# Contrast adjustment in one pass over 48 images: equal 32 KB rows, six buffers, two hardware DMA queues, a sum shared by two engines and a clip in two chunks

## The chip, the cores and the metric

The kernel runs on one core of a Trainium2 chip; the other cores were not part of the program. The metric is the device time of one execution in microseconds (us), lower is better. A profiled execution gives a span, which is about 1.8 us shorter than the measured time (238.6 us against 240.4 us).

## The reference

```python
x: (16, 3, 512, 512) float32, uniform random in 0..1        # 48 images of 1 MB, 50.33 MB
mean = np.mean(x, axis=(2, 3), keepdims=True)
return np.clip(mean + factor * (x - mean), 0, 1).astype(np.float32)      # factor = 1.5
```

Every image has to be read whole before its first output can be computed. So 50.33 MB come in and 50.33 MB go out, and between load and store an image stays on chip.

## The kernel before

A tile holds four images: 128 partitions with 8192 float32 each, so that one row of the DMA is 32 KB. The last two tiles hold two images, with rows of 16 KB. VectorE sums each row, a small matmul with a block matrix adds the rows of one image and spreads `(1 - factor) * mean`, ScalarE forms `relu(factor * x + bias)`, VectorE takes the minimum with 1, and the tile is stored from where it lies. A framework orders the instructions and places the waits.

```python
TILE_IMGS = [4] * 11 + [2, 2]
X_BUFS = 5
...
    for i, N in enumerate(TILE_IMGS):
        ...
        nc.sync.dma_start(out=xt, in_=src)                       # load: SP's hardware queue
        nc.vector.tensor_reduce(out=rsum, in_=xt, axis=X, op=add)
        nc.tensor.matmul(pbias, blockw[N], rsum, start=True, stop=True)
        nc.scalar.copy(out=bias, in_=pbias)
        nc.scalar.activation(out=xt, in_=xt, func=Relu, bias=bias, scale=factor)
        nc.vector.tensor_scalar(out=xt, in0=xt, scalar1=1.0, scalar2=None, op0=min)
        nc.gpsimd.dma_start(out=dst, in_=xt)                     # store: Pool's software queue
```

## Time and profile before

| | before |
|---|---|
| time, median of the first 3 runs | 240.37 us (240.05 to 240.52) |
| span of the profiled execution | 238.6 us |
| VectorE busy, ScalarE busy | 156.5 us (66%), 89.1 us (37%) |
| bytes by DMA | 100.66 MB, 422 GB/s over the span |

The first view is the page of the kernel before. The span is cut into 40 equal slices; the digits are the busy share of a slice in tenths, and the last line gives GB/s by slice. Below come the two DMA queues (packets, MB, share of 16 engines' time) and the costliest instructions (count | busy us, mean ns | idle us before them, and what ended it).

```profile
DVE  0088999999599079459629909917945979742300
ACT  2002966472906601900920650470190095406000
DMA  7999999999999999999999999999999999999995
GB/s 269 434 439 439 439 439 352 439 434 439 439 439 439 439 434 434 423 428 412 423 439 439 434 439 439 439 439 439 434 428 426 426 404 428 431 434 439 428 434 214
...
q1 hardware_dynamic: 1872, 50.33, 49.4%
q0 software_dynamic: 1872, 50.33, 49.0%
...
L77 DVE TENSOR_REDUCE rsum<-xt 128x1 f32<-128x8192 f32 (+1 forms) x13 | 104.4, 8029 | 61.7 <-DMA xt<-in_x_dram 61.7
L90 ACT ACTIVATE xt<-xt,bias 128x8192 f32<-128x8192 f32 (+1 forms) x13 | 85.8, 6598 | 0.4
L97 DVE TENSOR_SCALAR xt<-xt 128x8192 f32<-128x8192 f32 (+1 forms) x13 | 53.2, 4091 | 5.0 <-ACT xt L90 5.0
```

The row to read is DMA: 9 in all but the first and the last slice. VectorE and ScalarE have gaps, and VectorE's are ended by loads. The waits of the DMA queue on SP say what the loads themselves wait for, namely stores, which free the buffers:

```profile
SPq L74 <- DMA out_dram<-xt: 186.4, 8, 58.2
```

The packet records of the trace sharpen this. A row of 32 KB is one packet there; its median duration is 1.213 us in both directions, which makes 16 x 32,768 B / 1.213 us = 432 GB/s. The first data packet starts at 1.75 us, the last ends at 236.81 us, and all packet durations together make 234.74 us per engine. So the DMA is full from end to end.

In the timeline of one tile in the steady state (start, duration, instruction), the order on VectorE is sum of tile t+1, then clip of tile t:

```profile
162.37 8.69 DVE L77 TENSOR_REDUCE rsum<-xt 128x1 f32<-128x8192 f32 x1 [6.34 <-DMA xt<-in_x_dram]
170.97 4.42 DVE L97 TENSOR_SCALAR xt<-xt 128x8192 f32<-128x8192 f32 x1
175.69 0.53 POOL L104 DMA_DIRECT2D out_dram<-xt  x1 [18.83 <-DVE xt L97]
```

The clip and store belong to the tile that landed one period (19.4 us) earlier: a tile is on chip for about 33 us between landing and store.

### The profile page before, as it was taken

Reading aid. Unit: us, or ns where it says so; the run is one execution under the profiler, and the core shown is the slowest. Engines: PE = TensorE matmul, PEld = TensorE weight load, DVE = VectorE, ACT = ScalarE, POOL = GpSimd, SP = SyncE. Lnnn points to the kernel's source line nnn. Section 1 sums busy time; section 2 is a strip of 40 time slices with the busy share of each in tenths; the row PEclk is TensorE's granted clock in tenths of the full one; section 3 lists DMA queues with packets and bytes.
Section 4 is the critical chain, followed back from the end, with each engine's and each line's share of the span. In section 5 each row is a group of like instructions: output and inputs, shape, how many; then the busy total and the mean of one; then the engine's idle time right before and its main releaser. Section 6 shows DMA issues by size and latency. Waiting matters only on the chain.

```text
span 238.6 us, 238 instructions
## 1 busy us (share of the span) xinstructions
PE 7.4 (3%) x26; PEld 6.5 (3%) x26; DVE 156.5 (66%) x26; ACT 89.1 (37%) x27; POOL 10.3 (4%) x25
## 2 busy tenths in 40 slices
PE   0000000000000000000000000000000000000000
PEld 0000000000000000000000000000000000000000
DVE  0088999999599079459629909917945979742300
ACT  2002966472906601900920650470190095406000
POOL 2000001000000000000000000000000000500000
DMA  7999999999999999999999999999999999999995
GB/s 269 434 439 439 439 439 352 439 434 439 439 439 439 439 434 434 423 428 412 423 439 439 434 439 439 439 439 439 434 428 426 426 404 428 431 434 439 428 434 214
DMA packets 3744, 100.66 MB, mean 422 GB/s; under 512 B 416, under 2 KB 416, under 8 KB 416
## 3 DMA queue, kind: packets, MB, share of 16 engines
q1 hardware_dynamic: 1872, 50.33, 49.4%
q0 software_dynamic: 1872, 50.33, 49.0%
HBM read 50.33 MB, written 50.33 MB: 422 GB/s over the span
## 4 chain that ended last, share of the span: by engine, by line
issue 38%; DMA 35%; DVE 18%; POOL 2%; POOLq 0%; SPq 0%
DMA xt<-in_x_dram 19%; DMA out_dram<-xt 16%; DVE rsum L77 11%; DVE xt L97 7%; POOL out_dram L104 2%; POOLq L137 0%; SPq L74 0%; POOLq L104 0%
## 5 line engine op out<-in xcount | busy, mean ns | idle before, releaser
L77 DVE TENSOR_REDUCE rsum<-xt 128x1 f32<-128x8192 f32 (+1 forms) x13 | 104.4, 8029 | 61.7 <-DMA xt<-in_x_dram 61.7
L90 ACT ACTIVATE xt<-xt,bias 128x8192 f32<-128x8192 f32 (+1 forms) x13 | 85.8, 6598 | 0.4
L97 DVE TENSOR_SCALAR xt<-xt 128x8192 f32<-128x8192 f32 (+1 forms) x13 | 53.2, 4091 | 5.0 <-ACT xt L90 5.0
L88 ACT COPY bias<-pbias 128x1 f32<-128x1 f32 x13 | 2.1, 160 | 130.6 <-PE pbias L85 130.6
L104 POOL DMA_DIRECT2D out_dram<-xt x13 | 9.0, 692 | 213.0 <-DVE xt L97 212.8
L85 PE MATMUL pbias<-rsum,blockw 128*128 128x1 f32 x26 | 7.4, 355 | 209.5 <-DVE rsum L77 209.5
L85 PEld LDWEIGHTS pbias<-rsum,blockw 128*128 128x128 f32 x26 | 6.5, 311 | 210.3 <-DVE rsum L77 107.1
L88 ACT ACT_TABLE_LOAD x1 | 1.3, 1283 | 0.8 <-PEq L123 0.8
L51 POOL MEMSET blockw<- 32x32 f32 (+1 forms) x6 | 0.8, 128 | 0.2
L49 POOL MEMSET blockw<- 128x128 f32 x2 | 0.3, 205 | 0.3 <-POOLq L123 0.3
L123 POOL MEMSET const-float32-0.0<- 128x1 f32 x1 | 0.1, 104 | 0.2 <-issue 0.2
L123 POOL MEMSET const-bfloat16-1.0<- 128x1 bf16 x1 | 0.1, 113 | 0.0
L123 POOL MEMSET const-uint8-127<- 128x1 uint8 x1 | 0.1, 113 | 0.0
L123 POOL MEMSET const-float32-1.0<- 128x1 f32 x1 | 0.1, 110 | 0.0
## 6 DMA issues: line engine op xcount, KB each, us to landing
xt<-in_x_dram SPq DMA_DIRECT2D x11, 4096.0 KB, 24.6
out_dram<-xt POOLq DMA_DIRECT2D x11, 4096.0 KB, 36.0
xt<-in_x_dram SPq DMA_DIRECT2D x2, 2048.0 KB, 19.5
out_dram<-xt POOLq DMA_DIRECT2D x2, 2048.0 KB, 19.1
```

The costliest lines, as they stand in the source:

```text
L49: nc.gpsimd.memset(wt, 0.0)
L51: nc.gpsimd.memset(wt[b * PPI : (b + 1) * PPI, b * PPI : (b + 1) * PPI], wconst)
L77: nc.vector.tensor_reduce(out=rsum, in_=xt, axis=mybir.AxisListType.X, op=mybir.AluOpType.add,)
L85: nc.tensor.matmul(pbias, blockw[N], rsum, start=True, stop=True)
L88: nc.scalar.copy(out=bias, in_=pbias)
L90: nc.scalar.activation(out=xt, in_=xt, func=mybir.ActivationFunctionType.Relu, bias=bias, scale=factor,)
L97: nc.vector.tensor_scalar(out=xt, in0=xt, scalar1=1.0, scalar2=None, op0=mybir.AluOpType.min,)
L104: store_eng.dma_start(out=dst, in_=xt)
L123: nc = _bacc.Bacc("TRN2", target_bir_lowering=False, num_devices=1)
```

## The change

The intent is to shorten each tile's stay on chip and to take Pool's software queue out of the path: the sum is shared (4352 columns on VectorE, 3840 on ScalarE at the same time), the scale and the clip overlap in two chunks, the stores go out by ScalarE's hardware queue, six buffers replace five, all tiles are equal, and the order of instructions is fixed by hand (`manual_schedule`). The diff, cut to its core:

```diff
-TILE_IMGS = [4] * 11 + [2, 2]
-X_BUFS = 5
+ROW = 8192
+BUFS = 6
+CHUNKS = (5120, 3072)
+SUM = 4352
...
-        nc.vector.tensor_reduce(out=rsum, in_=xt, axis=X, op=add)
-        nc.tensor.matmul(pbias, blockw[N], rsum, start=True, stop=True)
-        nc.scalar.copy(out=bias, in_=pbias)
-        nc.scalar.activation(out=xt, in_=xt, func=Relu, bias=bias, scale=factor)
-        nc.vector.tensor_scalar(out=xt, in0=xt, scalar1=1.0, scalar2=None, op0=min)
-        nc.gpsimd.dma_start(out=dst, in_=xt)
+        nc.vector.tensor_reduce(out=sums[:, 0:1], in_=xt[:, 0:SUM], axis=X, op=add)
+        nc.scalar.activation(out=junk, in_=xt[:, SUM:ROW], func=Copy, accum_out=sums[:, 1:2])
+        nc.tensor.matmul(pbias, blockw, sums[:, 1:2], start=True, stop=False)
+        nc.tensor.matmul(pbias, blockw, sums[:, 0:1], start=False, stop=True)
+        nc.vector.tensor_copy(out=bias, in_=pbias)
+        for n in CHUNKS:
+            part = xt[:, c : c + n]
+            nc.scalar.activation(out=part, in_=part, func=Relu, bias=bias, scale=factor)
+            nc.vector.tensor_scalar(out=part, in0=part, scalar1=1.0, scalar2=None, op0=min)
+            c += n
+        nc.scalar.dma_start(out=dram(out_f, t), in_=xt)
...
+    with tc.manual_schedule():
+        for t in range(min(BUFS, n_tiles)):
+            load(t)
+        for t in range(n_tiles):
+            compute(t)
+            store(t)
+            if t + BUFS < n_tiles:
+                load(t + BUFS)
```

More of the change, by code (lines that the diff above doesn't have):

```diff
@@ L5 @@
 import concourse.tile as tile
-from concourse import bass_utils, mybir
+from concourse import mybir
 from concourse._compat import with_exitstack
-TILE_IMGS = [4] * 11 + [2, 2]
-X_BUFS = 5
-STORE_ENGINE = "gpsimd"
+P = 128
+ROW = 8192
+BUFS = 6
+CHUNKS = (5120, 3072)
+SUM = 4352
 @with_exitstack
@@ L23 @@
     nc = tc.nc
-    P = 128
+    f32 = mybir.dt.float32
+    Alu = mybir.AluOpType
+    Act = mybir.ActivationFunctionType
     B, C, H, W = x.shape
-    n_img = B * C
-    n_pix = H * W
+    n_img, n_pix = B * C, H * W
+    ppi = n_pix // ROW
+    per_tile = P // ppi
+    n_tiles = n_img // per_tile
+    assert ppi * ROW == n_pix and per_tile * n_tiles == n_img
     factor = float(factor)
-    f32 = mybir.dt.float32
-    assert sum(TILE_IMGS) == n_img
-    NMAX = max(TILE_IMGS)
+    wconst = (1.0 - factor) / float(n_pix)
@@ L36, with dram @@
     x_f = x.rearrange("b c h w -> (b c h w)")
     out_f = out.rearrange("b c h w -> (b c h w)")
-    wconst = (1.0 - factor) / float(n_pix)
+    def dram(ap, t):
+        return bass.AP(tensor=ap.tensor, offset=t * P * ROW, ap=[[ROW, P], [1, ROW]])
     consts = ctx.enter_context(tc.tile_pool(name="consts", bufs=1))
-    blockw = {}
-    for N in sorted(set(TILE_IMGS)):
-        wt = consts.tile([P, P], f32, name=f"blockw{N}")
-        PPI = P // N
-        if N == 1:
-            nc.gpsimd.memset(wt, wconst)
-        else:
-            nc.gpsimd.memset(wt, 0.0)
-            for b in range(N):
-                nc.gpsimd.memset(wt[b * PPI : (b + 1) * PPI, b * PPI : (b + 1) * PPI], wconst)
-        blockw[N] = wt
@@ L54 @@
-    xpool = ctx.enter_context(tc.tile_pool(name="xpool", bufs=X_BUFS))
-    rpool = ctx.enter_context(tc.tile_pool(name="rpool", bufs=12))
-    bpool = ctx.enter_context(tc.tile_pool(name="bpool", bufs=12))
-    psum = ctx.enter_context(tc.tile_pool(name="psum", bufs=8, space=bass.MemoryType.PSUM))
-    if STORE_ENGINE == "sync":
-        store_eng = nc.sync
-    elif STORE_ENGINE == "act":
-        store_eng = nc.scalar
-    else:
-        store_eng = nc.gpsimd
-    pix_off = 0
-    for i, N in enumerate(TILE_IMGS):
-        FREE = n_pix * N // P
-        npix_tile = n_pix * N
-        xt = xpool.tile([P, NMAX * n_pix // P], f32, name="xt")[:, :FREE]
-        src = bass.AP(tensor=x_f.tensor, offset=pix_off, ap=[[FREE, P], [1, FREE]])
-        dst = bass.AP(tensor=out_f.tensor, offset=pix_off, ap=[[FREE, P], [1, FREE]])
-        nc.sync.dma_start(out=xt, in_=src)
-        rsum = rpool.tile([P, 1], f32)
+    xpool = ctx.enter_context(tc.tile_pool(name="xpool", bufs=BUFS))
@@ new lines, with load @@
+    jpool = ctx.enter_context(tc.tile_pool(name="jpool", bufs=1))
+    rpool = ctx.enter_context(tc.tile_pool(name="rpool", bufs=2))
+    bpool = ctx.enter_context(tc.tile_pool(name="bpool", bufs=2))
+    psum = ctx.enter_context(tc.tile_pool(name="psum", bufs=2, space=bass.MemoryType.PSUM))
+    blockw = consts.tile([P, P], f32, name="blockw")
+    nc.gpsimd.memset(blockw, 0.0)
+    for a in range(0, P, ppi):
+        nc.gpsimd.memset(blockw[a : a + ppi, a : a + ppi], wconst)
+    tiles = {}
+    def load(t):
+        xt = xpool.tile([P, ROW], f32, name="xt")
+        nc.sync.dma_start(out=xt, in_=dram(x_f, t))
+        tiles[t] = xt
@@ L77, with compute @@
+    def compute(t):
+        xt = tiles[t]
+        sums = rpool.tile([P, 2], f32, name="sums")
         nc.vector.tensor_reduce(
-            out=rsum,
-            in_=xt,
-            axis=mybir.AxisListType.X,
-            op=mybir.AluOpType.add,
-        )
-        pbias = psum.tile([P, 1], f32)
-        nc.tensor.matmul(pbias, blockw[N], rsum, start=True, stop=True)
-        bias = bpool.tile([P, 1], f32)
-        nc.scalar.copy(out=bias, in_=pbias)
+            out=sums[:, 0:1], in_=xt[:, 0:SUM], axis=mybir.AxisListType.X, op=Alu.add
+        )
+        junk = jpool.tile([P, ROW - SUM], f32, name="junk")
@@ L90 @@
         nc.scalar.activation(
-            out=xt,
-            in_=xt,
-            func=mybir.ActivationFunctionType.Relu,
-            bias=bias,
-            scale=factor,
-        )
-        nc.vector.tensor_scalar(
-            out=xt,
-            in0=xt,
-            scalar1=1.0,
-            scalar2=None,
-            op0=mybir.AluOpType.min,
-        )
-        store_eng.dma_start(out=dst, in_=xt)
-        pix_off += npix_tile
+            out=junk, in_=xt[:, SUM:ROW], func=Act.Copy, accum_out=sums[:, 1:2]
+        )
@@ new lines, in compute @@
+        pbias = psum.tile([P, 1], f32, name="pbias")
+        nc.tensor.matmul(pbias, blockw, sums[:, 1:2], start=True, stop=False)
+        nc.tensor.matmul(pbias, blockw, sums[:, 0:1], start=False, stop=True)
+        bias = bpool.tile([P, 1], f32, name="bias")
+        nc.vector.tensor_copy(out=bias, in_=pbias)
+        c = 0
+        for n in CHUNKS:
+            part = xt[:, c : c + n]
+            nc.scalar.activation(out=part, in_=part, func=Act.Relu, bias=bias, scale=factor)
+            nc.vector.tensor_scalar(out=part, in0=part, scalar1=1.0, scalar2=None, op0=Alu.min)
+            c += n
@@ L110, with store @@
+    def store(t):
+        nc.scalar.dma_start(out=dram(out_f, t), in_=tiles.pop(t))
+    with tc.manual_schedule():
[6 more added lines that the diff above has]
+                load(t + BUFS)
 _INS = ['x', 'factor']
```

## The prediction

> **What bounds the kernel now.** The DMA engines, nearly all of the time. The 40 slices show them 90% or more busy in 38 slices, at 404 to 439 GB/s in nearly all of them; the page's mean is 422 GB/s for 100.66 MB. In the trace's packet records the first data packet starts at 1.8 us of the 238.6 us span and the last ends at 236.8 us, and between 20 us and that end the 16 engines are 100% busy. The 32 KB packets take 1.213 us (median) in both directions: 16 x 32,768 B / 1.213 us is 432 GB/s. All packets together take 234.7 us per engine, so the DMA has no bubble to give back. VectorE is busy 156.5 us (66%), ScalarE 89.1 us (37%). In the waits, VectorE waits 61.7 us for loads, and the load queue 186.4 us for stores to free buffers.
>
> **What the change does.**
> - Sum: the VectorE reduce of 8192 columns (8.69 us) becomes 4352 columns (about 4.6 us, scaled) beside a ScalarE copy-with-sum of 3840 columns (about 3.5 us, from 7.12 us for 8192 and 3.71 us for 4096). Clip: ScalarE about 4.6 and 2.9 us, VectorE about 2.8 and 1.7 us, partly overlapped. VectorE falls to about 9.4 us per tile, ScalarE rises to about 11. Before, a tile's clip stood behind the next tile's sum, so it waited for the next load; now it follows its own sum. Landing to store issue falls from about 34 us in steady state to about 15 (estimated from these durations). This is off the critical path: the DMA needs 19.4 us per tile (load plus store).
> - Six buffers for five: only a deeper backlog.
> - Stores move from the Pool software queue to ScalarE's hardware queue. The Trainium skill, DMA: Bandwidth & Descriptors, "Issuing engines are not separate DMA queues", says that DMAs of all issuers interleave on the same 16 engines, so there is no bandwidth to gain; the trace agrees, the two queues sharing 49.4% and 49.0%. Where the software queue's first store starts, at 37 to 39 us, some 27 load packets take 0.1 to 0.7 us longer, about 0.8 us per engine. This may go.
> - Tail: the two small tiles go; the last is 4 MB. After its load lands (about 208 us) the DMA has about 18 us of waiting stores, and its compute takes about 15 us. I expect no bubble, but only 2 to 3 us of slack.
>
> **Predicted.** Floor: 3,072 packets x 1.213 us / 16 = 232.9 us, plus 1.8 us of start, about 0.8 us of slow first packets and semaphore packets, 1.8 us of end, and 1.75 us between span and measured time: 239.0 us. With part of the odd delays left: 239.4 us, range 238.0 to 241.6. Chances: faster by over 2% 0.03, within 2% 0.92, slower by over 2% 0.05.
>
> **What would show it.** Packets again 1.213 us and engines 100% busy from 20 us to 2 us before the end (right); VectorE near 115 us and ScalarE near 135 us busy; load queue still waiting for stores; store time to landing falling from 36 us, and the stretch at 37 to 39 us without long packets. Wrong: an idle DMA stretch before the last store, or a packet time other than 1.213 us.
>
> **What would make it wrong.** Two hardware queues not sharing packet by packet: if stores are favoured, the backlog is gone when the last load lands and its 15 us of compute shows as up to 10 us of idle DMA. ScalarE stalling while issuing a store. Packets shorter with both directions from hardware queues would make it faster.

## The result and the profile after

The changed kernel takes 240.26 us (median of 6 runs, 239.88 to 240.53) and the kernel before 240.20 us (6 runs). The ratio is 1.0002, with a 95% interval of 0.9986 to 1.0018: the same time. A ratio here is the mean time of one kernel's fast runs over that of the other's fast runs of the same rounds, so it is not quite the ratio of the medians.

The page of the changed kernel, in the same rows as before:

```profile
DVE  0070946919377174372642825617437264282500
ACT  2058678596775744671790592574467169059200
DMA  7999999999999999999999999999999999999994
GB/s 269 434 439 439 434 357 439 423 439 439 439 434 428 417 439 423 428 428 434 439 439 434 439 439 439 428 430 423 434 428 423 434 434 439 439 434 439 434 439 198
...
q1 hardware_dynamic: 1728, 50.33, 49.5%
q10 hardware_dynamic: 1728, 50.33, 48.9%
...
L85 ACT ACTIVATE xt<-xt,bias 128x5120 f32<-128x5120 f32 (+1 forms) x24 | 87.7, 3701 | 22.1 <-DVE bias L81 14.7
L86 DVE TENSOR_SCALAR xt<-xt 128x5120 f32<-128x5120 f32 (+1 forms) x24 | 54.1, 2293 | 56.2 <-ACT xt L85 56.2
L70 DVE TENSOR_REDUCE sums<-xt 128x1 f32<-128x4352 f32 x12 | 56.2, 4684 | 47.5 <-DMA xt<-in_x_dram 47.5
L74 ACT ACTIVATE junk<-xt 128x3840 f32<-128x3840 f32 x12 | 40.8, 3403 | 68.2 <-DMA xt<-in_x_dram 61.4
```

Everything about the compute changed: VectorE fell from 156.5 to 111.9 us of busy time, ScalarE rose from 89.1 to 130.9 us. The DMA rows are nearly the same; one detail moved: the one weak slice of the first half, 352 GB/s in slice 7, has become 357 GB/s in slice 6. The load queue still waits for stores:

```profile
SPq L64 <- DMA out_dram<-xt: 145.1, 6, 50.1
```

The timeline of the last tile shows the shorter chain: sum at 209.09 us, store issued at 223.83 us, 14.7 us in all.

```profile
209.09 4.68 DVE L70 TENSOR_REDUCE sums<-xt 128x1 f32<-128x4352 f32 x1 [4.66 <-DMA xt<-in_x_dram]
209.15 3.40 ACT L74 ACTIVATE junk<-xt 128x3840 f32<-128x3840 f32 x1 [6.51 <-DMA xt<-in_x_dram]
...
214.70 7.31 ACT L85 ACTIVATE xt<-xt,bias 128x5120 f32<-128x5120 f32 x2 [2.06 <-issue]
219.29 4.50 DVE L86 TENSOR_SCALAR xt<-xt 128x5120 f32<-128x5120 f32 x2 [4.68 <-ACT xt L85]
223.83 0.34 ACTq L90 DMA_DIRECT2D out_dram<-xt  x1
```

In the packet records, this last tile's load ends at 207.5 us (the program sees it landed, by its semaphore, at 209.1 us), and the store before it still has packets until 227.3 us, so those 14.7 us are hidden behind waiting stores. The packets take 1.213 us again, together 234.87 us per engine (before 234.74).

### The profile page after: what moved, and what is told of

Its sections match the earlier page's. It is cut to its first block, busy times and chain, and to the rows that moved or that the text cites. A ratio compares the mean times of both kernels' runs of the same rounds, so it can differ in the third digit from the quotient of the medians.

```text
span 238.6 us, 306 instructions
## 1 busy us (share of the span) xinstructions
PE 14.0 (6%) x48; PEld 12.0 (5%) x48; DVE 111.9 (47%) x48; ACT 130.9 (55%) x49; POOL 0.9 (0%) x9
## 3 DMA queue, kind: packets, MB, share of 16 engines
q1 hardware_dynamic: 1728, 50.33, 49.5%
q10 hardware_dynamic: 1728, 50.33, 48.9%
## 4 chain that ended last, share of the span: by engine, by line
DVE 43%; ACT 24%; another core or an unknown queue 14%; DMA 5%; issue 4%; PE 2%; ACTq 0%
ACT xt L85 23%; DVE xt L86 23%; DVE sums L70 20%; DMA xt<-in_x_dram 5%; PE pbias L79 2%; ACT junk L74 1%; DVE bias L81 1%; PE pbias L78 0%; ACTq L90 0%; ACTq L85 0%; ACTq L74 0%
## 5 line engine op out<-in xcount | busy, mean ns | idle before, releaser
L85 ACT ACTIVATE xt<-xt,bias 128x5120 f32<-128x5120 f32 (+1 forms) x24 | 87.7, 3701 | 22.1 <-DVE bias L81 14.7
L86 DVE TENSOR_SCALAR xt<-xt 128x5120 f32<-128x5120 f32 (+1 forms) x24 | 54.1, 2293 | 56.2 <-ACT xt L85 56.2
L70 DVE TENSOR_REDUCE sums<-xt 128x1 f32<-128x4352 f32 x12 | 56.2, 4684 | 47.5 <-DMA xt<-in_x_dram 47.5
L74 ACT ACTIVATE junk<-xt 128x3840 f32<-128x3840 f32 x12 | 40.8, 3403 | 68.2 <-DMA xt<-in_x_dram 61.4
L78 PE MATMUL pbias<-sums,blockw 128*128 128x1 f32 x24 | 7.0, 361 | 196.4 <-ACT junk L74 196.4
L78 PEld LDWEIGHTS pbias<-sums,blockw 128*128 128x128 f32 x24 | 6.0, 311 | 197.3 <-ACT junk L74 180.5
L79 PE MATMUL pbias<-sums,blockw 128*128 128x1 f32 x24 | 7.0, 362 | 3.9 <-DVE sums L70 3.8
L79 PEld LDWEIGHTS pbias<-sums,blockw 128*128 128x128 f32 x24 | 6.0, 311 | 5.0 <-DVE sums L70 4.7
L81 DVE COPY bias<-pbias 128x1 f32<-128x1 f32 x12 | 1.9, 158 | 8.1 <-PE pbias L79 8.1
L74 ACT ACTIVATION_READ_ACCUMULATOR junk<-xt 128x1 f32 x12 | 2.2, 186 | 0.0
L58 POOL MEMSET blockw<- 32x32 f32 x4 | 0.5, 117 | 0.2
## 6 DMA issues: line engine op xcount, KB each, us to landing
out_dram<-xt ACTq DMA_DIRECT2D x12, 4096.0 KB, 36.9
```

Source lines behind the costliest of these rows:

```text
L58: nc.gpsimd.memset(blockw[a : a + ppi, a : a + ppi], wconst)
L70: nc.vector.tensor_reduce(out=sums[:, 0:1], in_=xt[:, 0:SUM], axis=mybir.AxisListType.X, op=Alu.add)
L74: nc.scalar.activation(out=junk, in_=xt[:, SUM:ROW], func=Act.Copy, accum_out=sums[:, 1:2])
L78: nc.tensor.matmul(pbias, blockw, sums[:, 1:2], start=True, stop=False)
L79: nc.tensor.matmul(pbias, blockw, sums[:, 0:1], start=False, stop=True)
L81: nc.vector.tensor_copy(out=bias, in_=pbias)
```

## The experiments

Two derived quantities are used below, both from the packet records. "Packet work" is the sum of all durations divided by 16 engines. "Excess" is the part of it above the median: the sum of (duration - 1.213 us) over the packets of a stretch, divided by 16. The packets of an engine overlap by 3 to 4 ns in these records, so that the work can come out slightly above the time from first to last packet (copy_only: 234.80 us in 234.47 us). Each result has the ratio to the kernel before and its interval.

Theory A: the 16 DMA engines set the time of both kernels, and compute is free as long as a backlog of stores hides it. Rivals: (B) a gain of the new queue or of the faster chain was cancelled by a loss elsewhere; (C) compute below 19.4 us per tile is hidden whatever its order.

### No compute at all

```diff
         for t in range(n_tiles):
-            compute(t)
             store(t)
```

> The changed kernel without any compute: each 4 MB tile is stored as it was loaded (a wrong result on purpose). Theory A, the 16 DMA engines alone set the time of both kernels: same, 239.5 to 240.6 us, 32 KB packets of 1.213 us again. Rival B, a gain of the change was cancelled by a loss in compute latency or at the tail: without compute faster than both by more than 2%, below 235.5 us.

Measured: 239.37 us (ratio 0.9972, 0.9947 to 0.9996). Its output is wrong, which doesn't matter for the time. The slices of this copy:

```profile
DMA  7998999999999999999999999999999999999996
GB/s 265 442 419 375 442 442 442 442 431 403 431 425 431 442 442 442 442 442 442 419 408 431 425 436 442 442 442 442 442 436 408 425 431 419 442 442 442 442 442 265
```

The median is 0.13 us below the expected band, but without any arithmetic this traffic takes as long, within 0.3% (0.5% at the end of the interval). B falls, as there is no compute loss of 2% that could cancel anything. A weak stretch (419 and 375 GB/s, from 12 to 24 us) sits where the first store starts, here much earlier.

### The queues exchanged, in each kernel

In the kernel before, ScalarE issues the stores (before_hw_store):

```diff
-STORE_ENGINE = "gpsimd"
+STORE_ENGINE = "act"
```

> The kernel before with its stores issued by ScalarE (hardware queue) and nothing else changed. Theory A: same, 239.6 to 240.6 us, and the stretch of long load packets at the first store stays, since the changed kernel has it too (about 0.9 us per engine at 28 us), so it belongs to the start of the stores and not to the software queue. Rival B, the queue is worth something that the rest of the change loses: faster by 1 us or more, and no long packets.

In the changed kernel, Pool issues them (after_sw_store):

```diff
-        nc.scalar.dma_start(out=dram(out_f, t), in_=tiles.pop(t))
+        nc.gpsimd.dma_start(out=dram(out_f, t), in_=tiles.pop(t))
```

> The changed kernel with its stores issued by Pool (software queue). Theory A: same, 239.8 to 241 us, long packets at the first store as in the other kernels. Rival B: slower by 1 us or more.

after_sw_store: 240.00 us (ratio 1.0001, 0.9978 to 1.0025), as expected. before_hw_store: 271.71 us (ratio 1.1335, 1.1296 to 1.1374), a clear miss of mine. Its slices have holes, and its timeline on ScalarE and VectorE shows where they come from:

```profile
DMA  8999999899999999999299899999159999701997
...
113.34 21.15 ACT L90 ACTIVATE xt<-xt,bias 128x8192 f32<-128x8192 f32 x3
133.91 17.60 ACTq L104 DMA_DIRECT2D out_dram<-xt  x3
151.56 0.22 ACT L88 COPY bias<-pbias 128x1 f32<-128x1 f32 x2 [17.07 <-DVE xt L97]
```

Moving the stores made the framework's scheduler bunch ScalarE's work: three scales in a row, then three stores in a row. The last of the three stores waits for a clip on VectorE (`<-DVE xt L97`), and with it ScalarE stands for 17.07 us, in which no tile is scaled. I had not looked at the order of instructions.

To part the queue from the order, the same kernel was written with the order fixed by hand (before_hw_ordered): on VectorE as before, on ScalarE each store behind the scale of its own tile.

```diff
+    with tc.manual_schedule():
+        for t in range(X_BUFS):
+            load(t)
+        sum_(0); scale(0)
+        for t in range(n_tiles):
+            if t + 1 < n_tiles: sum_(t + 1)
+            finish(t)                             # clip and store of tile t
+            if t + X_BUFS < n_tiles: load(t + X_BUFS)
+            if t + 1 < n_tiles: scale(t + 1)
```

> The kernel before with stores on ScalarE's hardware queue, like before_hw_store (271.7 us), but with the order of instructions fixed by hand to that of the kernel before on VectorE (sum of tile t+1, then clip of tile t), and on ScalarE each store directly behind the scale of its own tile. Theory A, the 271.7 us came from the scheduler's other order, in which ScalarE stands at two or three stores in a row and no clip starts meanwhile: 239.6 to 241 us. Rival D, issuing stores from ScalarE costs that much when one tile is clipped behind the sum of the next: again about 270 us.

Measured: 239.62 us (ratio 0.9977, 0.9948 to 1.0007). So the 32 us were the order, and D falls; the hardware queue itself shows no gain and no cost here beyond the noise. That fits the Trainium skill, "DMA: Bandwidth & Descriptors", section "Issuing engines are not separate DMA queues": DMAs of all issuers interleave on the same 16 engines. The traces agree: 49.5% and 48.9% for two hardware queues, 49.4% and 49.0% for a hardware and a software queue.

### The two halves of the shorter chain, undone one at a time

The whole sum on VectorE (after_serial_sum):

```diff
-    out=sums[:, 0:1], in_=xt[:, 0:SUM], axis=X, op=Alu.add
+    out=sums[:, 0:1], in_=xt, axis=X, op=Alu.add
-    nc.scalar.activation(out=junk, in_=xt[:, SUM:ROW], func=Act.Copy, accum_out=sums[:, 1:2])
-    nc.tensor.matmul(pbias, blockw, sums[:, 1:2], start=True, stop=False)
-    nc.tensor.matmul(pbias, blockw, sums[:, 0:1], start=False, stop=True)
+    nc.tensor.matmul(pbias, blockw, sums[:, 0:1], start=True, stop=True)
```

> The changed kernel with the whole sum on VectorE (one reduce of 8192 columns, no ScalarE sum, one matmul). One tile then takes about 18.7 us from landing to store issue, in series, still less than the 19.4 us of DMA per tile. Theory A with a serial chain: 13.3 us for the first load, 12 x 18.7 us, then the last store alone, about 12.5 us to the end: span about 249, time about 250.5 us, with the DMA idle in the last part, so slower by about 4%. Rival C, compute under 19.4 us per tile is always hidden: same, 240 us.

Measured: 250.27 us (ratio 1.0427, 1.0399 to 1.0456); C falls. Its slices and the end of its timeline:

```profile
DVE  0095695695695695695695695695694694694600
DMA  7999999999999999999999999999999999877077
...
217.31 8.68 DVE L69 TENSOR_REDUCE sums<-xt 128x1 f32<-128x8192 f32 x1
217.43 0.34 ACTq L84 DMA_DIRECT2D out_dram<-xt  x1
...
231.46 4.50 DVE L80 TENSOR_SCALAR xt<-xt 128x5120 f32<-128x5120 f32 x2 [4.63 <-ACT xt L79]
235.99 0.34 ACTq L84 DMA_DIRECT2D out_dram<-xt  x1
```

The last load ends at 203.3 us in the packet records, but the last two stores are issued at 217.43 and 235.99 us, one tile's chain (18.6 us) apart. A store takes only about 10 us when it has the DMA alone, so the DMA runs dry between them: the 0 in the slices. VectorE is only 64% busy in this run, and yet the kernel is bound by the serial chain sum, matmul, scale, clip. The kernel before has the same long sum and is not slowed, because there the sum of tile t+1 runs beside the scale of tile t. The shared sum thus repairs what the strict order by tile would cost.

The clip in one chunk (after_one_chunk):

```diff
-CHUNKS = (5120, 3072)
+CHUNKS = (8192,)
```

> The changed kernel with the clip in one chunk of 8192 columns; the sum stays split. Landing to store issue becomes about 17.2 us (4.7 + 0.9 + 7.1 + 4.4). Theory A: 12 x 17.2 us in series end before the DMA does, and waiting stores just cover the last tile: 239.8 to 241 us, same. Rival: the chunks are worth their 2.7 us per tile, at the tail at least: 242.5 us or more.

Measured: 243.36 us (ratio 1.0123, 1.0089 to 1.0158), so the rival was right here: the chunks are worth about 3 us to this kernel. The packet records say where the time goes. Packet work rises from 234.87 to 237.39 us, and the excess of the load packets from 1.59 to 4.09 us. The added excess sits at the starts of stores (summed over one or two neighbouring slices of 4 us):

```
store's first packet at us:     34.6   54.0   73.5   93.2  112.6  132.3  151.8  171.5  191.0
excess in the slices there, us:   0.83   0.29   0.49   0.26   0.49   0.16   0.33   0.28   0.21
```

Why each of these starts costs something is not shown. The stores don't come late: the second was issued at 47.48 us, 6.5 us before its first packet, and every later one of the table waited about 9 us or more. Nor does every change from one store to the next cost it: in the changed kernel (chain of 14.7 us) only the first store shows such an excess, 0.92 us, and in copy_only, whose stores follow one another too, only the first, 0.97 us. What is shown is that the longer chain brings these longer load packets. The rest of the loss is at the end: work up by 2.52 us, but the time from first to last packet by 2.98 us (235.71 to 238.69). Some 0.3 us of that is idle time of the engines before the last store's first packet at 228.38 us: the waiting stores no longer quite cover the last tile. I had left out the first effect altogether.

### The small tiles at the end

```diff
-TILE_IMGS = [4] * 11 + [2, 2]
+TILE_IMGS = [4] * 12
```

> The kernel before with twelve tiles of four images, without the two small tiles at the end. Theory A: when the last load lands (about 201 us) there are about 16 us of waiting stores, the next store is issued at about 214 us and the last at about 222 us, so the DMA stays busy: 239.8 to 241 us. Rival: the small last tiles are what keeps the tail short: slower by 4 us or more.

Measured: 239.61 us (ratio 0.9971, 0.9942 to 1.0000), 0.2 us below the expected band but level with the copy. The small tiles bought nothing in the kernel before, because stores were waiting at its end anyway.

### The depth of buffers

```diff
-BUFS = 6
+BUFS = 3        # after_bufs3; 4 in after_bufs4
```

> The changed kernel with 3 buffers in place of 6. Theory A: the depth of buffers is what lets a backlog of stores build up; with 3 of them each load waits for a store two tiles back, loads come in spurts, and the DMA runs dry while the last tile is computed: a hand simulation of the two queues, packet by packet with the durations of the trace, gives 250 us (and 240 us for 4 to 6 buffers), so slower by about 4%. Rival: three buffers (load, compute, store) are enough: 240 to 242 us.

> The changed kernel with 4 buffers in place of 6. Theory A, the hand simulation of the two queues: from 4 buffers on, the DMA never runs dry: 239.6 to 241 us. Rival: each buffer counts, so somewhere between the 248.5 us of 3 buffers and 240 us, above 242 us.

Measured: 3 buffers 248.52 us (ratio 1.0344, 1.0299 to 1.0389); 4 buffers 242.12 us (ratio 1.0077, 1.0050 to 1.0103, one slow run of 246.23 us left out). With 3 the theory holds; with 4 it missed its 241 us, and the rival (above 242 us) was right. The slices with 3 buffers:

```profile
DMA  7999997999999999999999999999999999999487
GB/s 272 443 448 448 406 374 342 411 395 390 427 427 427 427 459 438 427 427 427 432 438 432 432 443 427 427 427 428 427 438 443 432 395 400 438 432 427 182 379 304
```

There is a hole before the last store, as the hand simulation had it: the engines are idle for 4.1 us on average. But that is about half of the loss; the packet work is also 3.1 us higher than in the changed kernel (237.99 against 234.87 us), and 0.9 us more is idle near 42 us. With 4 buffers it put the hole at zero, and it was 2.9 us (DMA share 0.65 and 0.63 in the two 4 us stretches from 224 us, packets cut at the stretch's ends). The packet records point to the reason; the simulation was not run again with it. The first store was issued at 28 us, but its first packet starts at 32.3 us, not 0.9 us later as I had assumed. With 4 buffers the fifth load waits for this store, so the load queue is empty from 52.2 to 57.7 us; stores fill that time, and they are then missing at the end, where the last load lands about 5 us later than with 6 buffers (packets to 212.4 us against 207.5). So the fifth or sixth buffer is worth about 2 us to the changed kernel. Five buffers were not tried in it.

### Smaller rows, and what they laid open

```diff
-ROW = 8192
-BUFS = 6
-CHUNKS = (5120, 3072)
-SUM = 4352
+ROW = 4096
+BUFS = 12
+CHUNKS = (2560, 1536)
+SUM = 2176
```

> The changed kernel with rows of 16 KB (24 tiles of 2 MB, 12 buffers, sum and chunks halved too). Theory A: only the DMA counts, and a 16 KB packet took 0.611 us in the trace of before, two of them 9 ns more than one of 32 KB: 6,144 x 0.611 / 16 = 234.6 us of packets for 232.9 us, so 1 to 2 us slower than the changed kernel, 240.5 to 242.5 us. Rival: the first tile lands 5 us earlier and the last store is half as long, so faster than before.

Measured: 261.27 us (ratio 1.0881, 1.0860 to 1.0903). Both theories missed. The packets are as expected (0.611 us; packet work 237.2 us, of which 0.4 us are semaphore packets and about 2.1 us excess), but the DMA is only 61% busy from 205 to 258 us. The slices, and ScalarE's stores in a window of the timeline:

```profile
DMA  7999999999999999999999999999999954476347
...
80.99 2.41 DVE L70 TENSOR_REDUCE sums<-xt 128x1 f32<-128x2176 f32 x1
87.16 0.34 ACTq L90 DMA_DIRECT2D out_dram<-xt  x1
87.60 1.80 ACT L74 ACTIVATE junk<-xt 128x1920 f32<-128x1920 f32 x1 [7.53 <-DMA xt<-in_x_dram]
...
167.04 0.34 ACTq L90 DMA_DIRECT2D out_dram<-xt  x1
175.60 0.34 ACTq L90 DMA_DIRECT2D out_dram<-xt  x1
```

At 80.99 us the clip was done (VectorE begins the next sum then), yet the store is issued only at 87.16 us, and ScalarE stands with it. From 72 to 117 us the stores are 14.6 us apart; later on, from 150 us, they come every 8.55 us. What ended the waits stands in the semaphore records. A DMA signals its end on a semaphore, and in this kernel all 48 DMAs use eight of them. The store issued at 87.16 us signals on one whose previous DMA, a load of a later tile, completed at 87.1 us; the next one, issued at 101.75 us, on one whose previous DMA completed at 101.7 us. The instruction records of ScalarE have a wait for exactly that semaphore in front of each of these two stores; it ends at 87.12 and at 101.71 us. The kernel before uses sixteen, eight for loads and eight for stores. With twelve loads queued at once, a store gets a semaphore that a load deep in the other queue still holds. The compute then falls behind, and when the loads are done (194 us) the stores still come at 8.55 us each, where the DMA alone needs about 5 us for one.

The same kernel with its stores on Pool's queue, which brings the other eight semaphores back (after_row16k_sw):

```diff
-        nc.scalar.dma_start(out=dram(out_f, t), in_=tiles.pop(t))
+        nc.gpsimd.dma_start(out=dram(out_f, t), in_=tiles.pop(t))
```

> The kernel of 16 KB rows (261.3 us with both queues in hardware), with its stores issued by Pool, so on semaphores of their own. Theory S: the 261 us came from completion semaphores, of which the two hardware queues share eight; each store stood until a load deep in the other queue, an earlier user of its semaphore, had landed, and ScalarE stood with it. Without that sharing only the packets count, 6,144 x 0.611 / 16 = 234.6 us: 240.5 to 242.5 us. Rival P: 16 KB rows or 24 small tiles cost that much by themselves: again above 255 us.

Measured: 242.28 us (ratio 1.0091, 1.0071 to 1.0112); its semaphore records show sixteen again, and its slices are full:

```profile
DMA  7999999999999999999999999999999999999995
```

P falls. The edit also spares ScalarE the wait for the clip that goes before each store, but that wait is not the cause: it is part of the 8.55 us period of the late stretch, which is below the 9.7 us that load and store of such a tile need. What the 16 KB rows and 24 small tiles cost by themselves is 0.9% against the kernel before.

The changed kernel with 32 KB rows has the same sharing in small: from 103 to 151 us three stores wait for the landing of a load.

```profile
103.13 4.51 DVE L86 TENSOR_SCALAR xt<-xt 128x5120 f32<-128x5120 f32 x2 [4.69 <-ACT xt L85]
112.28 4.69 DVE L70 TENSOR_REDUCE sums<-xt 128x1 f32<-128x4352 f32 x1 [4.64 <-DMA xt<-in_x_dram]
112.33 0.34 ACTq L90 DMA_DIRECT2D out_dram<-xt  x1
```

The clip ends at 107.64 us, and the store is issued at 112.33 us, right after the landing at 112.28 us. Those 4.7 us cost no time there, as the DMA had other stores to move.

### Everything harmless put together

The hand-ordered version of before with ScalarE's queue, twelve equal tiles and six buffers (best_combo):

```diff
-TILE_IMGS = [4] * 11 + [2, 2]
-X_BUFS = 5
+TILE_IMGS = [4] * 12
+X_BUFS = 6
```

> A version put together of what cost nothing: the kernel before with its order fixed by hand, stores on ScalarE's queue, twelve equal tiles and six buffers. Theory A: there is nothing left to win but the odd delays of under 1 us; copying alone took 239.4 us: 239.3 to 240 us, ratio to before 0.996 to 1.000. Rival: the parts add up to a gain over 1%: below 237.5 us.

Measured: 239.85 us (ratio 0.9994, 0.9964 to 1.0024). The parts were not quite harmless together. In the profiled run (241.16 us, the slowest of the six, which range from 238.94 us) the DMA row has a dip before the last store:

```profile
DMA  7999999999999999999999999999999999999796
```

The engines are idle for 1.9 us there. ScalarE's store of tile 11 of 12 waits for its clip, and the scale of the last tile stands behind it: it starts at 215.42 us and the last store is issued at 227.04 us. In before_big_tail, where Pool issues the stores, these are 209.65 and 221.53 us. So in this run two changes that each cost nothing used up the slack at the end together; the other runs were not profiled.

No version beats the two kernels by an amount that these runs could show; the copy took 239.37 us with these tiles and queues, and other shapes of transfer than those above were not tried.

## Why the prediction was right

- **The bound.** Right: full DMA before and after, packets of 1.213 us in both, and a copy without arithmetic within 0.3%.
- **No gain from queues or from the shorter chain.** Right, shown by after_sw_store, before_hw_ordered and copy_only. The pieces of the chain were 4.68, 3.40 (plus 0.19 for reading the sum out), 4.56, 2.84, 2.83 and 1.76 us, against estimates of 4.6, 3.5, 4.6, 2.9, 2.8 and 1.7 us.
- **The tail with 2 to 3 us of slack.** Right: the last load landed at 209.1 us (predicted about 208), no bubble followed, and a chain 2.5 us longer (after_one_chunk) just began to show one (0.3 us).
- **The size.** 239.4 us was predicted, 240.26 us measured. The term that was mis-sized is "about 0.8 us per engine" of long load packets at the first store, which I ascribed to the software queue and expected to be partly gone. They came again with the hardware queue: 0.92 us of excess at 28 to 36 us (before: 0.70 us at 36 to 44 us), also in copy_only (0.97 us) and before_hw_ordered (0.79 us), and with Pool's queue in after_sw_store (0.90 us). So they go with the first store beside running loads, not with the kind of queue. after_one_chunk has smaller ones at later stores too, where copy_only has none; why is not settled. As 0.4 us for odd delays was already in the 239.4 us, they make some 0.5 us of the miss. The profiled run shows one more item that the sum had no term for: the 16 engines finish unequally, the last at 237.47 us, 1.3 us after their mean (0.2 us in after_sw_store). Both are small beside the scatter: the runs of the kernel before alone range from 239.47 to 240.97 us.
- **Store time to landing falling from 36 us.** Wrong: 36.9 us after. A faster chain doesn't shorten a queue that the DMA empties at its own pace; the stores just wait there.
- **Not foreseen.** The shared completion semaphores of the two hardware queues, which kept three tiles on chip for 19.4 us between landing and store where 14.8 us was the least, and that the strict order by tile makes the shared sum (10 us) and the chunks (3 us) necessary rather than gainful. The change took one hiding of compute, the overlap of neighbouring tiles, for another, a chain short enough to follow tile by tile.

## What to carry to other kernels

When the DMA row is full from end to end and the packet work nearly equals the span, run the kernel as a bare copy first: its time is the end of what any change to compute alone can win; other tiles or queues need a copy of their own. A part that is free in one structure may carry another: judge it by undoing it alone, as the shared sum was worth nothing in the total and 10 us inside the new kernel. Changes that are free one by one can share the same slack, as in the profiled run of best_combo. After moving a DMA to another engine, look at that engine's order of instructions and at which completion semaphores the queues now share, since an issue that waits holds up everything behind it.

## What the Trainium skill lacked or had wrong

- "DMA: Bandwidth & Descriptors", section "Where 436 GB/s comes from", says that for transfers between HBM and SBUF the HBM side binds, at about 358 GB/s per core; another section of the page has 425 GB/s for loads with the neighbouring core idle, and leaves about 358 GB/s to a core only when both stream. With this one core at work, slices show up to 439 GB/s of loads and stores together (whole packets, counted where they start), 60 to 180 us of the kernel before 435 GB/s, and the packets 432 GB/s; the 435 GB/s that the section gives for the fabric is what this case meets.
- The same page, section "Why a DMA increments its semaphore by 16 and not by 1", treats a semaphore shared by two DMAs in flight as a hazard for correctness only. None of the pages that I read has the cost in time where a framework avoids the hazard by waits: 261.27 us with eight shared semaphores and 242.28 us with sixteen.
- The same page, section "Issuing engines are not separate DMA queues", says that several issuers save only issue time. None of the pages that I read puts a number to what the issuer may lose: ScalarE stood 17.07 us at a group of stores in before_hw_store, which took 271.71 us.
- No page that I read has the cost of starting a stream of stores beside loads: 0.7 to 1.0 us of longer load packets per engine at the first store, and a first packet 4.3 us after the issue (28.0 to 32.3 us) in the changed kernel, where an idle DMA took 0.85 us (235.99 to 236.84 us, the last store of after_serial_sum).
